# Feed-forward blocks by seven half-size block products, and attention heads with query-major scores and a running-sum instruction, in a two-layer fp32 decoder trunk

## The chip, the cores and the metric

The kernel runs on one core of a Trainium2 chip. The metric is the time of one execution on the device in microseconds (us), the median of several runs. An engine here is one of the core's five: PE is TensorE (matmuls and transposes), DVE is VectorE, ACT is ScalarE, POOL is GpSimd, and SP is SyncE, which issues the loads of weights.

## The reference

Two layers, all in float32, on h of 512 rows and 1024 columns (mem has 256 rows):

```python
for l in range(DEPTH):
    h = h + 0.5 * swiglu_ffn(rms_norm(h, ffn1_norm[l]), ffn1_w_in[l], ffn1_w_out[l])
    h = h + hybrid_mixer(rms_norm(h, mix_norm[l]), w_in[l], conv_w[l], ...)
    h = h + memory_cross_attention(rms_norm(h, xattn_norm[l]), rms_norm(mem, mem_norm[l]), ...)
    h = h + 0.5 * swiglu_ffn(rms_norm(h, ffn2_norm[l]), ffn2_w_in[l], ffn2_w_out[l])
return rms_norm(h, final_norm)

def rms_norm(x, gain, eps=1e-6):
    return x * lax.rsqrt(jnp.mean(x * x, axis=-1, keepdims=True) + eps) * gain
def swiglu_ffn(x, w_in, w_out):            # w_in 1024 x 5632, w_out 2816 x 1024
    gate, up = jnp.split(x @ w_in, 2, axis=-1)
    return (jax.nn.silu(gate) * up) @ w_out
def stick_breaking_attention(q, k, v):     # 8 heads of 64, by blocks of 128 queries
    z = einsum('bhtd,bhsd->bhts', qb, kb) * 64 ** -0.5
    log_beta = log_sigmoid(z)
    log_1m_beta = where(causal, log_beta - z, 0.0)
    between = cumsum(log_1m_beta, axis=3, reverse=True) - log_1m_beta
    a = where(causal, exp(log_beta + between), 0.0)      # then a @ v
```

The mixer projects its input, runs the 8 stick-breaking heads and beside them 4 gated DeltaNet heads of 128 (a causal convolution and silu on q, k, v; l2-normalized q and k; a triangular solve in chunks; a state that goes from chunk to chunk), normalizes each head's output, gates the DeltaNet heads, and projects out.

## The kernel before

Everything lies transposed: columns of h on the partitions, 8 tiles h0 to h7 of 128 x 512. A float32 product is made of three matmuls: each operand is split into a high part (a cast on ScalarE, `split_act`, L164) and a low part (a subtraction on VectorE, `split_low`, L169), and `mm3` multiplies high by high, high by low and low by high. Weights come in units of 128 x 1024 (512 KB): `load` (L171) issues the transfer on SP's queue into one of three raw buffers `wraw`, `unit` (L178) makes the parts `whi` and `wlo` in one of four pairs of buffers, and `take` (L187) hands them to `products` (L199) in the order of a plan, one or more units ahead.

Each layer has four stages: feed-forward, mixer, cross-attention, feed-forward. The order of TensorE's instructions is fixed by the kernel: the stages are written as Python generators, and `weave` (L92) picks among them by a virtual clock. A generator's `yield 3400.0` says that its next part shall not be written before the clock has gone on by so many ns; `yield ("rb",)` waits for a mark; `mm` (L112) moves the clock. The order on the other engines is made by a scheduler, with the DeltaNet thread ahead of others (`urgent`).

*Feed-forward* (`ffn_dense`, L335). The hidden width of 2816 is 22 blocks of 128, in three groups of 8, 8 and 6 (`FGROUPS`). `gate_up` (L340) multiplies a gate unit and an up unit by the 8 tiles of x = h times gain, 512 columns wide. The root 1 / rms of each row is not in x; it is made meanwhile by `rms_rows` (L296) as a tile rb of 128 x 512 (a matmul of ones with the sum of squares, then `newton`, L218, three steps on 512 columns) and applied to the results:

```python
def gated(f, ps):                                            # L350
    nc.vector.tensor_tensor(gt, ps[0], self.rb, op=ALU.mult)     # L352
    nc.scalar.activation(gt, gt, AF.Silu)                        # L353
    nc.vector.tensor_tensor(m, ps[1], gt, op=ALU.mult)           # L355
    self.split_act(hi, m); self.split_low(lo, m, hi)
```

`down` (L367) multiplies a group's m by the 8 units of the output weights, and `add` (L361) scales by rb and adds to h. The next group's first block stands ahead of `down`.

*Mixer* (`mixer`, L912). Four threads share TensorE: the root, the DeltaNet heads one after another (`gdn_head`, L728), the attention heads in pairs (`sb_pair`, L583), and the projections (`mixer_dense`). A DeltaNet head is a chain of short steps on TensorE and VectorE: transposes of k, the root of its length (`rsqrt`, eleven small VectorE steps on 128 x 4), the scaled keys (L771), a triangular solve by levels (1 to 64), then four chunks (L857 on): the product with the state (`rhs`), the product with the solve's result X, its copy `yv` (L870), the new state (L880) and the output. The yields leave room in which the other threads' matmuls stand. An attention head is key-major: scores z lie with keys on the partitions; the sum over later keys is made by TensorE, with a triangle of -1 (`ntri`) and a block of -1 (`nones`, both in tile `cr`) times the split softplus, on top of z in the bank:

```python
t1 = max(z, 0) + Ln(1 + Exp(-|z|)); hi, lo = split(t1)           # scores, L621 to L624
mm(z[...], self.ntri if s2 == s else self.nones, part)           # sums, L630
a = Exp(z); aa = split(a); mm3(av, vpad, aa)                     # weights L642, values
```

*Cross-attention* stands behind the mixer; its memory part is normalized by `mem_norm` (L996) in a thread beside the first feed-forward.

Of the kernel before, what the change touches and what calls it, by code (L numbers as in the profile page):

```python
# [25 lines left out]
P = 128  # L26
# [26 lines left out]
class Trunk:  # L53
# [67 lines left out]
    def setup(self):  # L121
# [23 lines left out]
        self.cr = self.sb([P, 2, P], "cr", F32R)  # L145
        self.cb = self.sb([P, 3, P], "cb", BF16)
        self.ntri, self.nones = (self.cr[:, i, :] for i in range(2))
        self.nsb, self.ngd, self.idb = (self.cb[:, i, :] for i in range(3))
        nc.gpsimd.tensor_copy(self.ntri, stage[:, 0:P])
        nc.gpsimd.tensor_scalar(out=self.nones, in0=self.ones, scalar1=-1.0, scalar2=None, op0=ALU.mult)  # L150
# [36 lines left out]
    def take(self):  # L187

        self.held += 1
        while self.plan and len(self.ahead) < max(1, W_BUFS + 1 - self.held):  # L190
            self.ahead.append(self.unit(self.load(self.plan.pop(0))))
        return self.ahead.pop(0)
# [21 lines left out]
    def rsqrt(self, x, n, tag):  # L214

        return self.newton(x, *(self.sb([P, n], tag + c, bufs=2) for c in "ytm"))

# [92 lines left out]
    G_SLOTS = [f"s{i}" for i in (*range(12, 27), *range(31, 34))]  # L310


    @staticmethod
    def ffn_plan(w_in, w_out):
        r = []
        for i, (f0, f1) in enumerate(FGROUPS):
            if i:
                p0, p1 = FGROUPS[i - 1]
                r += [w_in[f0, 0], w_in[f0, 1]]
                r += [w_out[d][:, p0 * P:p1 * P] for d in range(KD)]  # L320
                f0 += 1
            r += [w_in[f, j] for f in range(f0, f1) for j in range(2)]
        return r + [w_out[d][:, f0 * P - P:f1 * P] for d in range(KD)]
# [3 lines left out]
    def ffn(self, layer, off, *beside, out=None):  # L327
# [5 lines left out]
        self.weave(self.rms_rows(("b6", "b7"), *waits), *beside, self.ffn_dense(x, out is not None))  # L333

    def ffn_dense(self, x, last):  # L335
        nc = self.nc
        banks = [f"b{i}" for i in range(6)]
        g, pend = {}, []

# [10 lines left out]
        def gated(f, ps):  # L350
            gt = self.slot(self.turn("gt", ("s2", "s3")))
            nc.vector.tensor_tensor(gt, ps[0], self.rb, op=ALU.mult)  # L352
            nc.scalar.activation(gt, gt, AF.Silu)  # L353
            m = self.slot(self.turn("m", ("s4", "s5")))
            nc.vector.tensor_tensor(m, ps[1], gt, op=ALU.mult)  # L355
# [4 lines left out]

        def add(d, p, cols=slice(0, S)):  # L361
            h = self.h[d][:, cols]
            t = self.slot(self.turn("up", ("s6", "s7")))[:, cols]
# [3 lines left out]
        def down(f0, f1):  # L367
            d = 0
            xs = [g[f] for f in range(f0, f1)]
            end = f1 == NF  # L370
            while d < KD:
                n = 1 if end and d >= KD - 2 else 2
# [13 lines left out]
                ps = yield from self.products(n, xs, banks)  # L386
# [4 lines left out]
                d += n  # L391

        done = None
        for f0, f1 in FGROUPS:
            yield from gate_up(f0)
            if done:
                yield from down(*done)
            for f in range(f0 + 1, f1):
                yield from gate_up(f)
            done = (f0, f1)  # L400
        yield from down(*done)
# [3 lines left out]
    def final(self, out):  # L405
# [7 lines left out]
        def row(i, r):  # L413
            b = self.bank("rms", banks)
            self.rows(b, r, nt=NT // 2)
            rb = self.slot(("s24", "s25")[i])[:, :S // 2]
# [81 lines left out]
    def gates(self, layer):  # L498
# [36 lines left out]
        yield 12800.0  # L535
# [45 lines left out]
    SBB = (((2, 0, 256),), ((1, 0, 384), (3, 384, 128)), ((0, 0, 512),))  # L581

    def sb_pair(self, layer, pair):  # L583
        nc = self.nc
        mm = self.mm
        t1s = ("s15", "s16", "s17")
        names = [f"s{i}" for i in range(19, 27)]
# [4 lines left out]
        hi, lo = (t.rearrange("p t (j d) -> p t j d", j=3)[:, :, 0:3:2, :] for t in self.vpad)  # L592
        self.split_act(hi, src)
# [674 lines left out]
```

## Time and profile before

| | |
|---|---|
| time, median of 3 runs | 2524.07 us (2523.88 to 2525.02) |
| the profiled execution | 2528.47 us, of which 2526.7 us span |
| mean granted TensorE clock | 0.996 |
| stages on PE, layer 0, from the span's start | 8.4 feed-forward, 373.7 mixer, 736.4 cross-attention, 900.5 feed-forward |
| layer 1 | 1261.5, 1624.0, 1984.9, 2148.6 |

Times in rows are us from the start of the span. "L118" is the matmul in `mm` and "L169" the subtraction in `split_low`, so groups are told apart by tiles: xh, xl are the normalized input's parts, whi and wlo the weights', `b` a PSUM bank (b0 to b5 in feed-forward; in the mixer b6 and b7 are the DeltaNet heads'), `s` a working tile, and f1i, f2o, ... the weights in memory. A busy matmul overlaps the one behind it, so the time that one costs in a run of equal ones is the run's length over their count.

### The profile page before, as it was taken

The numbers are of one execution on the slowest core, as the hardware profiler recorded it, in microseconds if no ns is written. First come the engines' busy times: TensorE is split into PE (matmuls) and PEld (weight loads), VectorE is DVE, ScalarE is ACT, GpSimd is POOL, SyncE is SP. The second block draws the span as 40 slices with busy tenths as digits, with TensorE's granted clock in tenths as the row PEclk, the third lists the DMA queues.
The fourth block names the chain that finished last, engine by engine and source line by source line (L and its number), as shares of the span: only waits on it lengthen the run. The fifth ranks groups of instructions, "written<-read, shape, count | busy, mean of one in ns | idle before, by whom it ended". The sixth has DMA issues, their size and how long they took to land.

```text
span 2526.7 us, 30844 instructions
## 1 busy us (share of the span) xinstructions
PE 2469.2 (98%) x12268; PEld 2070.6 (82%) x12268; DVE 1438.3 (57%) x2585; ACT 970.7 (38%) x1545; POOL 10.5 (0%) x21
## 2 busy tenths in 40 slices
PE   8999999999999999999999999999999999999997
PEld 6888887888889888888888888778888988888886
DVE  6443467788675563444554443687876755544345
ACT  4222236555544432222322222466555444322222
POOL 0000000000000000000000000000000000000000
PEclk9999999999999999999999999999999999999999
DMA  5223232111233123332323222311111432322322
GB/s 192 84 100 100 98 94 67 42 51 36 66 110 125 59 92 100 100 101 88 101 95 98 97 89 94 98 59 42 51 43 51 150 101 67 100 85 99 100 94 65
DMA packets 64672, 220.16 MB, mean 87 GB/s; under 512 B 7312, under 2 KB 9616, under 8 KB 64528
## 3 DMA queue, kind: packets, MB, share of 16 engines
q1 hardware_dynamic: 64096, 217.15, 26.5%
q8 instruction: 96, 1.57, 0.3%
q10 hardware_dynamic: 432, 1.04, 0.1%
q14 instruction: 48, 0.39, 0.0%
HBM read 216.07 MB, written 2.10 MB: 86 GB/s over the span
## 4 chain that ended last, share of the span: by engine, by line
PE 89%; DVE 8%; ACT 1%; issue 1%; DMA 0%; DVEq 0%; SPq 0%; ACTq 0%
PE b L118 88%; DVE wlo L169 2%; PE b L496 1%; DVE s L169 1%; ACT whi L164 1%; DVE qkv L713 1%; DVE s L624 0%; DVE s L810 0%; DVE qk L169 0%; DMA wraw<-f1i 0%; DVE s L822 0%; ACT s L164 0%; DVE s L835 0%; DVE s L836 0%; DVE s L429 0%
## 5 line engine op out<-in xcount | busy, mean ns | idle before, releaser
L118 PE MATMUL b<-xh,whi 128*128 128x512 f32 x2112 | 843.6, 399 | 10.1 <-ACT whi L164 8.4
L118 PE MATMUL b<-xh,wlo 128*128 128x512 f32 x2112 | 826.3, 391 | 0.0
L118 PE MATMUL b<-xl,whi 128*128 128x512 f32 x2112 | 825.7, 391 | 0.2
L164 ACT CAST whi<-wraw 128x1024 fp32r<-128x1024 f32 (+1 forms) x408 | 407.9, 1033 | 1033.5 <-PE b L118 947.6
L118 PE MATMUL b<-s,whi 128*128 128x512 f32 (+1 forms) x2136 | 591.6, 364 | 0.2 <-ACT whi L164 0.2
L169 DVE TENSOR_TENSOR wlo<-wraw,whi 128x1024 fp32r<-128x1024 f32 (+1 forms) x408 | 479.3, 1200 | 72.2 <-ACT whi L164 72.0
L118 PEld LDWEIGHTS b<-xh,whi 128*128 128x128 f32 x2112 | 398.7, 189 | 88.7 <-ACT whi L164 8.4
L118 PEld LDWEIGHTS b<-xh,wlo 128*128 128x128 f32 x2112 | 397.6, 188 | 84.8 <-DVE wlo L169 0.8
L118 PEld LDWEIGHTS b<-xl,whi 128*128 128x128 f32 x2112 | 398.6, 189 | 79.2 <-DVE xl L169 1.5
L118 PEld LDWEIGHTS b<-s,whi 128*128 128x128 f32 x2136 | 382.3, 188 | 64.5 <-issue 0.6
L118 PE MATMUL b<-s,wlo 128*128 128x512 f32 (+1 forms) x1068 | 387.1, 362 | 0.0
L352 DVE TENSOR_TENSOR s<-b,rb 128x512 f32<-128x512 f32 x88 | 60.7, 691 | 450.6 <-PE b L118 450.5
L118 PEld LDWEIGHTS b<-s,wlo 128*128 128x128 f32 x1068 | 201.2, 188 | 32.3
L364 DVE TENSOR_TENSOR s<-b,rb 128x512 f32<-128x512 f32 (+1 forms) x98 | 66.3, 680 | 224.8 <-PE b L118 224.7
L164 ACT CAST s<-s 128x512 fp32r<-128x512 f32 x186 | 107.4, 579 | 158.9 <-DVE s L355 124.6
L169 DVE TENSOR_TENSOR s<-s,s 128x512 fp32r<-128x512 f32 x186 | 118.3, 637 | 65.6 <-ACT s L164 65.2
L118 PEld LDWEIGHTS b<-s,s 128*128 128x128 f32 x656 | 84.6, 191 | 13.1 <-issue 8.1
L118 PE MATMUL b<-s,s 128*128 128x128 f32 (+2 forms) x656 | 86.7, 274 | 3.5 <-DVE rqt L224 1.8
L365 DVE SCALAR_TENSOR_TENSOR h<-s,h 128x512 f32<-128x512 f32 (+1 forms) x98 | 63.0, 673 | 0.0
L353 ACT ACTIVATE s<-s 128x512 f32<-128x512 f32 x88 | 54.9, 625 | 17.6 <-DVE s L352 17.6
L118 PE MATMUL b<-s,cr 128*128 128x128 f32 (+3 forms) x320 | 55.1, 311 | 6.6 <-DVE s L169 6.6
L355 DVE TENSOR_TENSOR s<-b,s 128x512 f32<-128x512 f32 x88 | 60.1, 684 | 1.6 <-ACT s L353 1.4
(240 smaller groups left out, 1820.3 us busy)
## 6 DMA issues: line engine op xcount, KB each, us to landing
wraw<-f1i SPq DMA_DIRECT2D x88, 512.0 KB, 3.7
wraw<-f2i SPq DMA_DIRECT2D x88, 512.0 KB, 3.7
wraw<-wi SPq DMA_DIRECT2D x56, 512.0 KB, 3.5
wraw<-f1o SPq DMA_DIRECT2D x32, 512.0 KB, 3.8
wraw<-xkv SPq DMA_DIRECT2D x32, 512.0 KB, 3.5
wraw<-f2o SPq DMA_DIRECT2D x32, 512.0 KB, 4.2
wraw<-wo SPq DMA_DIRECT2D x16, 512.0 KB, 3.5
wraw<-xq SPq DMA_DIRECT2D x16, 512.0 KB, 3.5
```

What stands on the lines that cost most here:

```text
L118: self.nc.tensor.matmul(out, lhsT, rhs, **kw)
L164: self.nc.scalar.copy(hi, src)
L169: self.nc.vector.tensor_tensor(lo, src, hi.bitcast(F32), op=ALU.subtract)
L352: nc.vector.tensor_tensor(gt, ps[0], self.rb, op=ALU.mult)
L353: nc.scalar.activation(gt, gt, AF.Silu)
L355: nc.vector.tensor_tensor(m, ps[1], gt, op=ALU.mult)
L364: nc.vector.tensor_tensor(t, p, self.rb[:, cols], op=ALU.mult)
L365: nc.vector.scalar_tensor_tensor(out=h, in0=t, scalar=0.5, in1=h, op0=ALU.mult, op1=ALU.add)
L496: self.nc.tensor.transpose(out, src, self.ident[:src.shape[0], :src.shape[0]])
L713: nc.vector.scalar_tensor_tensor(out=y, in0=cv[:, 1 + i:1 + i + S], scalar=w[i], in1=y, op0=ALU.mult, op1=ALU.add)
```

## The change

The feed-forward's input is now also built with the root inside. For blocks 0 to 4 (`WHOLE = 5`) the products are as before, with rb applied to the gate ahead of silu and again behind it. From block 5 on, a block's gate and up (2 x 128 rows of weights), the input's 1024 columns (two halves of 512) and the 512 rows of h (two halves of 256) are taken as a 2 x 2 matrix of blocks each, and the eight block products are made as seven, Strassen's scheme in Winograd's form: p1 = a11 b11, p2 = a12 b21, p5 = s1 t1, p6 = s2 t2, p7 = s3 t3, p3 = s4 b22, p4 = a22 t4. Each is 4 tiles x 3 matmuls of 256 columns. The sums s1 to s4 of weights are made per block on VectorE (`early`: L452 s1, L453 s2, L454 s3, L455 s4) and split; the sums t1 to t4 of the input once per feed-forward (`ffn_parts`). `period` writes product 1 and 2 of block f around products 7, 3 and 4 of block f - 1.

```diff
+    def ffn_parts(self, layer, off):
+        yield ("rb",)
+        for k in range(KD // 2):
+            for j, n in enumerate((n1, n2)):
+                stt(out=n, in0=self.h[k + 4 * j], scalar=self.gain(layer, off, k + 4 * j), in1=self.rb,
+                    op0=ALU.mult, op1=ALU.mult)
+            tt(t3[:, self.HALVES[k % 2]], n2[:, hi], n1[:, hi], op=ALU.subtract)
+            tt(n1[:, hi], n1[:, lo], n1[:, hi], op=ALU.subtract)
+            split(n1, "b11", "t1")
+            split(n2, "b21", "b22")
...
+            yield 3000.0
+        self.mark("parts", 3000.0)
...
+        def early(f):
+            (a11, a12), (a21, a22) = [(r[:, :half], r[:, half:]) for r in raw[f]]
+            hi, lo = self.part(raw[f][0])
...
+            tt(s12[:, :half], a21, a22, op=ALU.add)
+            tt(s12[:, half:], s12[:, :half], a11, op=ALU.add)
+            tt(s3, a11, a21, op=ALU.add)
+            tt(s4, s12[:, half:], a12, op=ALU.add)
+            raw[f] = s12, s3, s4, a22
...
+        def late(f):
+            hi, lo = self.part(raw[f][2], raw[f][3])
...
+        def product(f, left, right, out, start):
+            hi, lo = w[f][left]
+            for k, r in enumerate(self.parts[right]):
+                ks = slice(k * P, (k + 1) * P)
+                self.mm3(out, (hi[:, ks], lo[:, ks]), r, start and k == 0, k == KD // 2 - 1, skip=True)
+                yield 0
...
+        def p3(f):
+            yield from product(f, "s4", "b22", c, False)
+            tt(gt[:, second], c, snap[:, second], op=ALU.add)
+            nc.scalar.activation(gt, gt, AF.Silu)
+        def p4(f):
+            yield from product(f, "a22", "t4", a, False)
+            stt(out=m[:, second], in0=m[:, second], scalar=-1.0, in1=gt[:, second], op0=ALU.mult, op1=ALU.mult)
+            stt(out=m[:, first], in0=a, scalar=-1.0, in1=gt[:, first], op0=ALU.mult, op1=ALU.mult)
+            keep(f, m)
+        def period(f, before, more):
+            yield from p1(f)
+            if before:
+                yield from p7(f - 1)
+            sum3(f)
+            yield from p2(f)
+            if more:
+                early(f + 1)
+            yield from p5(f)
+            yield from p6(f)
+            if more:
+                sums12(f + 1)
+            if before:
+                yield from p3(f - 1)
+                yield from p4(f - 1)
+            late(f)
+            if self.plan and isinstance(self.plan[0], tuple):
+                fetch(f + 2)
         def add(d, p, cols=slice(0, S)):
...
-            nc.vector.tensor_tensor(t, p, self.rb[:, cols], op=ALU.mult)
-            nc.vector.scalar_tensor_tensor(out=h, in0=t, scalar=0.5, in1=h, op0=ALU.mult, op1=ALU.add)
+            stt(out=h, in0=p, scalar=0.5, in1=h, op0=ALU.mult, op1=ALU.add)
```

The root of the rows comes from `rms` instead of `rms_rows`: sums on [128, 4], `newton` there, and four matmuls that spread it to 128 x 512. `down` has product 7 of a group's last block ahead of it and products 3 and 4 behind the first six matmuls of its first unit.

In the mixer the scores are query-major, so that the sum over later keys runs along a row. One VectorE instruction makes it (a scan along reversed columns), a subtraction joins it to z, the weights are transposed on TensorE and split there, and `values` takes two matmuls per tile of keys, with the high and low parts of v side by side, instead of three. `rsqrt_log` takes the place of `rsqrt` in DeltaNet heads (rk, rq, ro) and in the attention heads' norms (sn). Many yields have other numbers.

```diff
+    def rsqrt_log(self, x, n, tag):
+        nc.scalar.activation(y, x, AF.Ln)
+        nc.scalar.activation(y, y, AF.Exp, scale=-0.5)
+        nc.vector.tensor_tensor(t, y, y, op=ALU.mult)
+        nc.vector.scalar_tensor_tensor(out=t, in0=t, scalar=-0.5, in1=x, op0=ALU.mult, op1=ALU.mult)
+        nc.vector.scalar_tensor_tensor(out=y, in0=t, scalar=1.5, in1=y, op0=ALU.add, op1=ALU.mult)
...
+            for t, c, width in bl:
+                back = slice(c + width - 1, c - 1 if c else None, -1)
+                nc.vector.tensor_tensor_scan(out=run[:, back], data0=self.ones[:, 0:1].to_broadcast([P, width]),
+                                             data1=t1[:, back], initial=0.0, op0=ALU.mult, op1=ALU.add)
+            nc.vector.tensor_tensor(t1, z[:, :w], run[:, :w], op=ALU.subtract)
+            nc.scalar.activation(t1, t1, AF.Exp)
...
-                    for part in sp[j, s2]:
-                        mm(z[:, c + (s2 - s) * P:c + width], self.ntri if s2 == s else self.nones, part,
-                           start=False, stop=True, skip_group_check=True)
...
+                    self.transpose(at[i][:, c2:c2 + P], raw[n][:, c + s * P:c + (s + 1) * P])
...
-        rk = self.rsqrt(ss, NT, "rk")
+        rk = self.rsqrt_log(ss, NT, "rk")
...
-            yield 2000.0 if n else 3400.0
+            yield 2200.0 if n else 4200.0
...
-            yield 200.0
+            yield 1000.0
```

VectorE in a feed-forward, before: all that it does for one block (wraw are the loaded weights, b4 and b5 the banks of gate and up, s22 and s23 the parts of m).

```order
L352 TENSOR_TENSOR s3_122_617<-b4_120_566,rb_64_265 128x512
L169 TENSOR_TENSOR wlo_128_629<-wraw_126_626,whi_127_628 128x1024
L169 TENSOR_TENSOR wlo_131_635<-wraw_129_632,whi_130_634 128x1024
L355 TENSOR_TENSOR s5_123_620<-b5_121_567,s3_122_617 128x512
L169 TENSOR_TENSOR s23_125_623<-s5_123_620,s22_124_622 128x512
```

The same engine in one period after (vv holds s1 and s2, vl holds s3, s31 and s32 hold s4; L493 and L508 are additions of two products, L514 and L515 make m):

```order
L165 TENSOR_TENSOR wlo_338_1863<-wraw_328_1811,whi_337_1862 128x1024
L452 TENSOR_TENSOR vv_339_1866<-wraw_329_1813 128x512
L454 TENSOR_TENSOR vl_340_1867<-wraw_328_1811,wraw_329_1813 128x512
L453 TENSOR_TENSOR vv_339_1866<-vv_339_1866,wraw_328_1811 128x512
L493 TENSOR_TENSOR s2_333_1818<-b3_331_1816,s6_332_1817 128x256
L455 TENSOR_TENSOR s31_341_1868<-vv_339_1866,wraw_328_1811 128x512
L508 TENSOR_TENSOR s3_313_1687<-b1_311_1685,s33_312_1686 128x256
L165 TENSOR_TENSOR wlo_343_1901<-vv_339_1866,whi_342_1900 128x1024
L514 SCALAR_TENSOR_TENSOR s5_314_1688<-s5_314_1688,s3_313_1687 128x256
L515 SCALAR_TENSOR_TENSOR s5_314_1688<-b0_310_1684,s3_313_1687 128x256
L165 TENSOR_TENSOR wlo_347_1937<-s32_321_1737,whi_346_1936 128x512
L165 TENSOR_TENSOR wlo_347_1937<-wraw_309_1682,whi_346_1936 128x512
```

Five rows have become fifteen; the low part of one block's a22 (the last row) stands eleven rows behind the sums of the next block. The last two rows' weights wraw_309 are of the block before wraw_328.

TensorE in the fourth DeltaNet head of layer 0, before, from its last level (b7_1070) to the first chunk's product (b6_1075); whi and wlo are units of a projection:

```order
L118 MATMUL b7_1070_5488<-s36_1050_5383,s39_1004_5139 128x128 x4
L118 MATMUL b1_1055_5398<-xh4_456_2576,whi_987_5064 128x512
L118 MATMUL b1_1055_5398<-xl4_457_2577,whi_987_5064 128x512
L118 MATMUL b1_1055_5398<-xh4_456_2576,wlo_988_5065 128x512
L118 MATMUL b1_1055_5398<-xh5_458_2580,whi_987_5064 128x512
L118 MATMUL b1_1055_5398<-xl5_459_2581,whi_987_5064 128x512
L118 MATMUL b1_1055_5398<-xh5_458_2580,wlo_988_5065 128x512
L118 MATMUL b1_1055_5398<-xh6_460_2584,whi_987_5064 128x512
L118 MATMUL b1_1055_5398<-xl6_461_2585,whi_987_5064 128x512
L118 MATMUL b1_1055_5398<-xh6_460_2584,wlo_988_5065 128x512
L118 MATMUL b6_1075_5519<-s32_1000_5120,s36_1050_5383 128x128
```

And after, the same head from its last levels (b7_1200 to b7_1205) through the first chunk (b6_1209 to b7_1214) to the attention head's transposes (L701):

```order
L118 MATMUL b7_1200_6390<-s18_1194_6354,s34_1139_6095 128x128 x4
L118 MATMUL b6_1202_6399<-s39_1145_6116,s36_1193_6353 128x128 x4
L118 MATMUL b7_1203_6405<-s36_1193_6353,s39_1145_6116 128x128 x4
L118 MATMUL b6_1204_6411<-s18_1194_6354,s34_1139_6095 128x128 x4
L118 MATMUL b7_1205_6417<-s36_1193_6353,s39_1145_6116 128x128 x4
L118 MATMUL b6_1209_6432<-s32_1141_6097,s36_1193_6353 128x128
L118 MATMUL b7_1211_6436<-yv_1210_6434,s31_1125_6024 128x128
L118 MATMUL b6_1213_6440<-yv_1210_6434,s35_1140_6096 128x128
L118 MATMUL b7_1214_6443<-st_1212_6438,qkv_976_5341 128x128
L701 MATMUL b2_1216_6447<-cst_13_91,s15_1187_6322 128x128
```

The nine projection matmuls between the last level and the first chunk are gone from there, and the steps of the head stand next to each other.

## Rows read from the trace of the kernel before

**Rows 1.** The page: busy time by engine; share of the chain that ended last.

```profile
PE 2469.2 (98%) x12268; PEld 2070.6 (82%) x12268; DVE 1438.3 (57%) x2585; ACT 970.7 (38%) x1545; POOL 10.5 (0%) x21
...
PE 89%; DVE 8%; ACT 1%; issue 1%; DMA 0%; DVEq 0%; SPq 0%; ACTq 0%
```

**Rows 2.** Windows: us, busy PE, PEld, DVE, ACT, POOL; clock, DMA share, GB/s.

```profile
373.70:736.40 362.70, 345.62 (x1958) 292.06 (x1957) 279.72 (x693) 204.25 (x386) 0.52 (x1) 0.99 0.18 56
900.50:1261.50 361.00, 361.00 (x1587) 297.88 (x1586) 168.27 (x209) 103.82 (x131) 0.00 (x0) 1.00 0.30 96
```

**Rows 3.** The chain in order of time: start, us, what; cross-attention and feed-forward.

```profile
767.07 2.86 PE b L118 x24
...
862.16 751.68 PE b L118 x3301
```

**Rows 4.** Timeline of DVE: start, us, line, operation, tiles, shapes.

```profile
100.69 2.36 DVE L169 TENSOR_TENSOR wlo<-wraw,whi 128x1024 fp32r<-128x1024 f32 x2 [0.21 <-ACT whi L164]
...
422.06 1.22 DVE L169 TENSOR_TENSOR wlo<-wraw,whi 128x1024 fp32r<-128x1024 f32 x1
423.19 0.75 DVE L800 TENSOR_TENSOR s<-b,s 128x256 f32<-128x256 f32 x2
423.86 0.42 DVE L814 TENSOR_TENSOR s<-b,s 128x256 f32<-128x256 f32 x1
...
485.11 0.69 DVE L902 TENSOR_TENSOR s<-s,roy 128x512 f32<-128x512 f32 x1
485.71 0.16 DVE L224 TENSOR_TENSOR rkt<-rky 128x4 f32<-128x4 f32 x1
```

**Rows 5.** Groups by form: busy us, mean ns of one, idle before them.

```profile
L164 ACT CAST whi<-wraw 128x1024 fp32r<-128x1024 f32 x376 | 382.7, 1050 | 953.2 <-PE b L118 872.1 <-issue 76.9 <-DMA wraw<-f1i 2.6
...
L624 DVE SCALAR_TENSOR_TENSOR s<-b,s 128x512 f32<-128x512 f32 x32 | 21.7, 679 | 4.1 <-ACT s L623 4.1
```

**Rows 6.** The page: DMA issues, KB each, median us from issue to landing.

```profile
wraw<-f1i SPq DMA_DIRECT2D x88, 512.0 KB, 3.7
...
wraw<-f2o SPq DMA_DIRECT2D x32, 512.0 KB, 4.2
```

**Rows 7.** Timeline of DVE: first gate after the root in the second-half feed-forward, layer 0.

```profile
919.36 0.69 DVE L352 TENSOR_TENSOR s<-b,rb 128x512 f32<-128x512 f32 x1
```

**Rows 8.** Windows in the first mixer: a wait near 408, one DeltaNet head.

```profile
407.00:411.00 4.00, 2.12 (x12) 1.62 (x11) 2.24 (x7) 3.95 (x4) 0.00 (x0) 0.91 0.30 120
481.00:551.40 70.40, 66.60 (x405) 57.39 (x403) 57.23 (x150) 40.10 (x82) 0.00 (x0) 1.00 0.14 46
```

**Rows 9.** Groups of PE by form, first mixer: the running sums (cr).

```profile
L118 PE MATMUL b<-s,cr 128*128 128x128 f32 x64 | 10.9, 263 | 2.6 <-DVE s L169 2.6
L118 PE MATMUL b<-s,cr 128*128 128x256 f32 x48 | 10.5, 300 | 0.0
L118 PE MATMUL b<-s,cr 128*128 128x384 f32 x32 | 8.9, 362 | 0.0
L118 PE MATMUL b<-s,cr 128*128 128x512 f32 x16 | 6.4, 471 | 0.7 <-DVE s L169 0.7
```

**Rows 10.** Timeline of PE; then the transposes' group by form.

```profile
104.34 0.61 PE L118 MATMUL b<-cst,mny 128*128 128x128 f32 x4
...
766.69 0.38 PE L496 MATMUL b<-cst,s 128*128 128x128 f32 x2
...
L496 PE MATMUL b<-cst,s 128*128 128x128 f32 x192 | 30.1, 274 | 1.1 <-DVE s L989 0.8
```

**Rows 11.** Timeline of DVE: one head's root of the keys.

```profile
483.27 0.17 DVE L220 TENSOR_SCALAR rky<-ss 128x4 int32<-128x4 int32 x1
...
489.13 0.16 DVE L226 SCALAR_TENSOR_TENSOR rky<-rkt,rky 128x4 f32<-128x4 f32 x1
```

**Rows 12.** Timeline of DVE: two steps of a head's chunks.

```profile
541.77 0.35 DVE L880 SCALAR_TENSOR_TENSOR st<-st,eg,b 128x128 f32<-128x128 f32 x1
...
544.92 0.28 DVE L870 COPY yv<-b 128x128 f32<-128x128 f32 x1
```

More of the change, by code (lines that the diff above doesn't have):

```diff
@@ new lines, in p1, with p2 @@
+        def p1(f):
+            a, bc = (self.bank("dense", banks) for _ in range(2))
+            a, b, c = a[:, first], bc[:, first], bc[:, second]
+            snap = self.slot(self.turn("snap", ("s33", "s6")))
+            gt, m = self.slot(self.turn("gt", ("s2", "s3"))), self.slot(self.turn("m", ("s4", "s5")))
+            st[f] = a, b, c, snap, gt, m
+            yield from product(f, "a11", "b11", a, True)
+            nc.scalar.copy(snap[:, first], a)
+        def p2(f):
+            a, b, c, snap, gt, m = st[f]
+            yield from product(f, "a12", "b21", b, True)
@@ new lines, in p5, with p6, p7 @@
+        def p5(f):
+            a, b, c, snap, gt, m = st[f]
+            yield from product(f, "s1", "t1", c, False)
+            nc.scalar.copy(m[:, second], c)
+            tt(gt[:, first], b, snap[:, first], op=ALU.add)
+        def p6(f):
+            a, b, c, snap, gt, m = st[f]
+            yield from product(f, "s2", "t2", a, False)
+            nc.scalar.copy(snap[:, second], a)
+        def p7(f):
+            a, b, c, snap, gt, m = st[f]
+            yield from product(f, "s3", "t3", a, False)
+            tt(m[:, second], a, m[:, second], op=ALU.add)
@@ L391, in down @@
                 d += n
-        done = None
-        for f0, f1 in FGROUPS:
[L395 to L401, printed above, removed]
+                if d == KD - 1 and not end:
+                    self.fill(1)
+                    fetch(left + 1)
+                    early(left + 1)
+        for f in range(self.WHOLE):
+            if f == self.WHOLE - 1:
+                fetch(f + 1)
+            yield from gate_up(f)
+        early(self.WHOLE)
+        sums12(self.WHOLE)
+        fetch(self.WHOLE + 1)
+        yield ("parts",)
+        f = self.WHOLE
+        for f0, f1 in FGROUPS:
+            if f0:
+                sums12(f)
+                fetch(f + 1)
+            end = min(f1, NF - 1)
+            f2 = f
+            while f2 <= end:
+                yield from period(f2, f2 > f, f2 < end)
+                f2 += 1
+            yield from down(f0, f1, end)
+            f = f2
     HALVES = (slice(0, S // 2), slice(S // 2, S))
@@ L645, in values @@
[L645 to L652 removed]
+            self.split_act(hi, at[n][:, :w])
+            self.split_low(lo, at[n][:, :w], hi)
```

289 lines of the change are left out of this document (171 added, 118 removed).

## The prediction

> **What bounds it now.** I read the page's busy times and chain first, then windows of each stage, then single timelines. TensorE works for 98% of the span and the chain of waits lies on it for 89% [rows 1]. Feed-forward stages have no gap at all: 361.00 us busy of 361.00, VectorE 168 us, ScalarE 104 us; a mixer has 345.6 of 362.7 [rows 2]. So a feed-forward stage is worth its matmuls times their spacing, as long as the other engines keep up; a mixer is nearly that, with small waits inside. The spacing is read where long runs of equal matmuls stand in the chain: 3301 of (nearly all) 512 columns in 751.68 us, 0.2277 us each, and 24 of 256 columns in 2.86 us, 0.1192 us each [rows 3]. A 256-column matmul costs 0.52 of a 512-column one, not 0.5. That is the first number which the change depends on.
>
> **The products.** Of the 22 blocks of a feed-forward, 17 change form. Before, a block is 2 x 8 x 3 = 48 matmuls of 512: 48 x 0.2277 = 10.93 us. After, it is 7 x 4 x 3 = 84 of 256: 84 x 0.1192 = 10.01 us. That is 0.92 us a block, and 4 x 17 = 68 blocks: **-62.4 us**. The down products keep their count. [...]
>
> **Does VectorE keep up?** It does the block sums of the weights and more low parts. One period's fifteen instructions (the order's piece shows twelve; the split of m, the add of product 7 and the low part of s3 follow): two of 1024 columns, eight of 512, five of 256. Back to back these take 1.14, 0.60 and 0.33 us from start to start (2.36 less the last one's 1.22; 485.11 to 485.71; 0.75 less 0.42) [rows 4], so 2 x 1.14 + 8 x 0.60 + 5 x 0.33 = 8.73 us of TensorE's 10.01. Laid out with its waits, VectorE stands idle for about 1.2 us per period, at the low part of [a11|a12]: that waits for ScalarE's cast of 1.05 us [rows 5], which may begin when product 2 has freed the weight buffer. The parts are early by some 3 us where TensorE wants them (a11 of the next block lies ready about 6.7 us into the period and is wanted at 10.0). ScalarE has 2 casts of 1024, 4 of 512, a Silu and 3 short copies, under 6 us.
>
> There is a second loop. The up-weights' buffer is held until the low part of a22, and the load into it feeds the next sums (L452) after that. From L452 to the end of a22's low part are 3 x 0.60 + 0.33 + 0.60 + 0.33 + 1.14 + 0.66 + 1.20 + 0.09 = 6.15 us, and a landing takes 3.7 us [rows 6]: 9.9 us against 10.01. Three loops thus stand within 15% of each other; TensorE's is the longest, by little, and the 3 us in hand cover a slightly longer one over runs of 4, 8 and 5 blocks between down products. I take no loss here, and keep the other end for a rival.
>
> **Ends of the feed-forward.** (a) The root for the rows is now made on [128, 4] and spread by four float32 matmul pairs, after four pairs for the sums; a pass costs 0.11 us, (0.61 less 0.27) / 3 [rows 10], so 16 x 0.11 = 1.8 us where the one 512-column pair took about 1.0: +0.8 x 4 = **+3**. (b) The right-hand parts must be built after the root: four rounds, about 4.9 us each on VectorE with their low parts, besides 2.4 us for each whole block's gate. In the built order, 25 to 28 us of VectorE's work stand between the root and the low part of the fifth block's weights. Before, the root was done 18.9 us into the second-half stage (919.36 less 900.5) [rows 2, 7]; after, about 2.5 us earlier, since 512-wide Newton steps go. So 16.5 + 28 = 44.5, wanted at 4 x 10.93 = 43.7. I take 1 to 1.5 us late in each: **+5**. (c) The last block's m is needed six matmuls (1.4 us) after its last product; two short VectorE steps, a cast and a low part are 0.66 + 0.62 + 0.69 + hops, 2.2 us: +0.8 x 4, with small change at the joins **+4**. Feed-forward together: -50.
>
> **The mixers.** Per mixer go the running sums on TensorE, 64, 48, 32 and 16 matmuls of 128, 256, 384 and 512 columns [rows 9]: 64 x 0.11 + 48 x 0.12 + 32 x 0.17 + 16 x 0.23 = 21.9 us, and 8 of each width in the values product, 5.0. 80 transposes come, 0.11 each (0.38 less 0.27) [rows 10]: 8.8. TensorE has **18 us less** to do. But what fills the time between the steps of the DeltaNet heads, one after another, is that same work. Counted in the built order at these spacings, before the first head stand 31.5 us, in the four heads 64.7, 64.0, 64.0, 64.0, and behind them 41.2; in the changed order 26.0, 71.1, 59.5, 64.3, 47.9 and 42.6. A head took 70.4 us with 64.0 of work, so 6.4 of waits [rows 8]. In the fourth head the filling ends early (the order's second piece). From its last levels on, the steps follow each other bare: matmul, 0.8 us to the copied or added result (a copy starts 0.15 us after its matmul ends and takes 0.28, an add 0.35 [rows 12]), three such per chunk, and 1.1 us behind each wide product. That half takes about 23 us; with its filling it took 30. So 16 us of filling taken there give back 7, and the last pair of attention heads, whose transposes, roots and scaling now stand behind the last chunk with nothing beside them, adds about 5.
>
> The roots give something. Before a head's scaled keys (L771) Newton's eleven small steps stand between long ones: from 483.27 to 489.13, 5.9 us, and L771 behind them releases the bank that TensorE waits for [rows 11]. Two ScalarE steps and three on VectorE are 5 instead of 11: I take 2 us a head, -8. With waits as before otherwise: 31.8 + 77.5 + 65.9 + 70.7 + 64.8 + 5 + 43.2 - 8 = 351 against 362.7. I take **-10 a mixer**, both -20.
>
> The scan is in no row. Its ends: 0.60 us for 512 columns, as any two-operand step (the maximum next to it takes 0.679 in all) [rows 4, 5], and 1.14, as a step of twice the columns. As each element needs the one before it, I take the upper end: 8 x (1.14 + 0.87 + 0.33 + 0.60) = 23.5 us a mixer, 10.6 more than at the lower. Beside it go 24 low parts and come 24 subtractions of equal size; the roots take off about as much as the merges add. VectorE's 57.2 of 70.4 us a head [rows 8] rises by some 3. [...]
>
> Sum: -62.4 + 3 + 5 + 4 - 20 = -70. The profiled execution took 2528.5 us (2526.7 of span), 4.4 above the median of 2524.1; 2524 - 70 = **2454 us**.
>
> **Rivals.**
> *The weights' loop binds.* If landings take 4.2 us, as one group does [rows 6], and the steps overlap no more than half (6.6 us), the period is 10.8: 0.8 x 68 less the 3.3 us in hand in each of 12 runs, about +15 to +30. For it: the loops' closeness. Against: loads are spaced, not in pairs. 2465 to 2495.
> *It binds hard, and the kernel is slower.* Place: L452 to a22's low part to the load. The gain of 70 is used up when 68 x e - 40 = 70, e = 1.6, a period of 11.6 us. At full durations (1.22, 0.69, 0.42) the loop is 7.0 us and VectorE's sum 10.06, so it needs landings over 4.6 us in all periods, where most rows say 3.7. 2530 to 2560.
> *The mixers give nothing, or lose.* If VectorE, with the long scans in one queue with the heads' short steps, delays each of these by half a microsecond, some 20 waits a head x 0.5 x 4 heads is 40 us a mixer in which half is hidden: +10 instead of -10. 2475 to 2500. TensorE's clock adds to it: after 2 us of waiting near 408 us its granted clock fell, 0.91 over that stretch [rows 8], and the bare tail waits more.
> [...]
>
> **Chances.** The forecast (2440 to 2470) 0.45; a soft loop 0.18; mixers giving nothing 0.22; faster than 2430 0.07; slower 0.06; within 0.2%, 5 us, which is what a measurement of this kernel can tell from no change, 0.02. From the cases: faster 0.92, same 0.02, slower 0.06. Range 2425 to 2500.
>
> **What would show it.** 256-column matmuls at 0.119 us in the block stretches with TensorE busy over 99%; a period of 10.0 us; VectorE at 85 to 90% there; waits at the fifth block of some us; a fourth head with TensorE idle for over 10 us. Wrong it would be by waits of TensorE for low parts inside the periods, by a load landing late at L452, or by scans ahead of the heads' steps.

## The result and the profile after

The changed kernel takes 2462.33 us (2460.1 to 2464.32, 4 runs) against 2523.98, a ratio of 0.9755 (95% interval 0.9738 to 0.9772). The forecast was 2454, its range 2425 to 2500.

The page of the changed kernel, busy time by engine and the chain's shares, against [rows 1]:

```profile
PE 2394.4 (97%) x14548; PEld 2115.5 (86%) x14548; DVE 1777.2 (72%) x3159; ACT 1182.3 (48%) x2035; POOL 9.1 (0%) x19
...
PE 86%; DVE 11%; ACT 1%; issue 1%; DMA 0%; DVEq 0%; ACTq 0%
```

TensorE has lost 75 us of busy time, VectorE has gained 339, and VectorE's share of the chain went from 8% to 11%. The windows of the changed kernel's stages say where the time came from; columns as in [rows 2].

```profile
8.60:366.90 358.30, 353.86 (x2220) 320.09 (x2221) 261.09 (x428) 169.28 (x266) 3.73 (x6) 1.00 0.33 111
366.90:713.00 346.10, 329.73 (x1845) 273.31 (x1844) 284.60 (x602) 195.31 (x394) 0.00 (x0) 0.99 0.17 58
...
877.20:1228.20 351.00, 348.75 (x2214) 316.84 (x2212) 249.03 (x395) 159.83 (x247) 0.00 (x0) 1.00 0.31 100
1228.20:1579.00 350.80, 348.36 (x2214) 316.78 (x2212) 253.91 (x408) 159.93 (x250) 2.08 (x4) 1.00 0.31 101
1579.00:1927.50 348.50, 332.31 (x1845) 274.84 (x1845) 283.48 (x600) 195.20 (x394) 0.00 (x0) 0.98 0.17 57
...
2091.10:2462.50 371.40, 354.17 (x2265) 323.71 (x2263) 255.27 (x434) 156.40 (x246) 2.82 (x4) 0.97 0.29 93
```

Taken from the stage starts of before, and for the last stage from the spans' ends, the feed-forwards gave 7.0, 10.0, 11.7 and 6.7 us, 35 in all where 50 were forecast. The mixers gave 16.6 and 12.4, 29 where 20 were forecast. Two terms were off by 15 and by 9, in opposite directions; that the sum lies within 9 us of the forecast is in part luck. The cross-attentions are the same within 0.1 us.

A period inside a run of seven-product blocks is read on VectorE's timeline:

```profile
1051.42 1.23 DVE L165 TENSOR_TENSOR wlo<-wraw,whi 128x1024 fp32r<-128x1024 f32 x1 [1.14 <-ACT whi L160]
1052.56 0.68 DVE L452 TENSOR_TENSOR vv<-wraw 128x512 f32<-128x512 f32 x1
...
1058.04 0.69 DVE L165 TENSOR_TENSOR wlo<-wraw,whi 128x512 fp32r<-128x512 f32 x1
...
1061.48 1.22 DVE L165 TENSOR_TENSOR wlo<-wraw,whi 128x1024 fp32r<-128x1024 f32 x1 [1.14 <-ACT whi L160]
1062.62 0.68 DVE L452 TENSOR_TENSOR vv<-wraw 128x512 f32<-128x512 f32 x1
```

From one L452 to the next are 10.06 us: 84 matmuls of 256 columns at 0.1198 each. VectorE's only gap in it is 1.14 us, ahead of the low part that waits for ScalarE's cast. From L452 to the end of a22's low part (1058.04 + 0.69) are 6.17 us. A landing took 3.1 us, by the DMA issues between 1050 and 1075 us:

```profile
wraw<-f2i SPq DMA_DIRECT2D x4, 512.0 KB, 3.1
```

So the loads' loop is 9.3 us long, and TensorE has no gap over three such periods, in which VectorE is busy for 89%:

```profile
1040.00:1070.00 30.00, 30.00 (x253) 30.00 (x252) 26.57 (x46) 18.07 (x30) 0.00 (x0) 1.00 0.29 105
```

At the entry of the blocks TensorE does wait. The chain in order of time in the last feed-forward, at the end of its last whole block and in the first products of the first seven-product block:

```profile
2139.84 9.15 PE b L118 x46
2148.99 0.02 issue
2149.01 0.37 ACT s L483
2149.39 0.54 ACT s L423
...
2149.95 0.69 DVE s L424
...
2151.16 0.69 DVE s L426
2151.85 0.60 DVE vl L454
2152.44 0.60 DVE s L455
...
2153.57 1.23 DVE wlo L165
```

L423 to L426 are the gate of the last whole block (silu, the second factor rb, the product with up); L453 to L455 are the weight sums of the first seven-product block, and the low part at the end is that of s1 and s2. The input's parts are not on this piece of the chain, but they stood ahead of it in VectorE's queue. They begin with L382, which needs the root, here in the second feed-forward (start 877.2) and in the last (start 2091.1):

```profile
896.17 0.75 DVE L382 SCALAR_TENSOR_TENSOR s<-h,gn,rb 128x512 f32<-128x512 f32 x1 [4.88 <-ACT rb L316]
...
2116.47 0.74 DVE L382 SCALAR_TENSOR_TENSOR s<-h,gn,rb 128x512 f32<-128x512 f32 x1
```

That is 19.0 and 25.4 us after the stage's start. From just before it VectorE works without a gap until the low part is done:

```profile
2114.20:2155.00 40.80, 36.88 (x177) 30.83 (x176) 40.77 (x69) 22.35 (x34) 0.00 (x0) 0.98 0.17 58
```

Windows around the entries, of the first, second and last feed-forward:

```profile
45.00:90.00 45.00, 41.31 (x237) 35.91 (x236) 41.28 (x80) 21.65 (x36) 0.00 (x0) 0.96 0.17 59
925.00:945.00 20.00, 18.56 (x116) 16.52 (x115) 18.39 (x28) 9.77 (x16) 0.00 (x0) 1.00 0.28 95
...
2150.00:2160.00 10.00, 6.08 (x30) 5.67 (x29) 9.26 (x14) 3.47 (x6) 0.00 (x0) 0.68 0.16 52
```

TensorE stands still for 3.7, 1.4 and 3.9 us there, and the granted clock of these stretches is 0.96 and 0.68 in the first and the last. Part of each ran at a granted clock of 0.50 (61.5 to 64.0 us and 2155.3 to 2160.1), with 512-column matmuls 0.427 us apart in the first, where they stood 0.227 apart ahead of the waits, and 256-column ones 0.213 apart in the last, against 0.1198. In the third feed-forward no such wait is listed.

In the mixer, windows from each DeltaNet head's first transposes to the next one's, and the stretch behind the fourth:

```profile
401.40:468.70 67.30, 65.81 (x385) 54.96 (x385) 60.39 (x121) 42.09 (x82) 0.00 (x0) 1.00 0.16 56
468.70:533.90 65.20, 62.57 (x377) 52.63 (x377) 59.71 (x129) 38.94 (x84) 0.00 (x0) 1.00 0.17 57
533.90:603.00 69.10, 68.01 (x410) 57.73 (x410) 59.44 (x130) 40.26 (x88) 0.00 (x0) 1.00 0.14 47
603.00:662.60 59.60, 52.37 (x314) 43.89 (x315) 48.07 (x111) 35.71 (x81) 0.00 (x0) 0.97 0.16 54
662.60:713.00 50.40, 46.47 (x205) 37.29 (x204) 31.02 (x55) 19.56 (x33) 0.00 (x0) 0.93 0.20 63
```

The first three heads take 65 to 69 us where one took 70.4 [rows 8]. The fourth is shorter, but TensorE stands for 7.2 us in it and 3.9 behind it, at a falling clock. The scan, by form on VectorE:

```profile
L828 DVE TENSOR_TENSOR_SCAN s<-cst,s 128x512 f32<-128x512 f32 x16 | 19.5, 1220 | 0.2
...
L828 DVE TENSOR_TENSOR_SCAN s<-cst,s 128x128 f32<-128x128 f32 x16 | 6.5, 406 | 0.0
```

1220 ns for 512 columns is what a subtraction of 1024 takes (1221 ns, L165), the upper end that the prediction took.

### The profile page after: what moved, and what is told of

It reads as the page before. It is cut to its first block, busy times and chain, and to the rows that moved or that the text cites. A ratio compares the mean times of both kernels' runs of the same rounds, so it can differ in the third digit from the quotient of the medians.

```text
span 2462.5 us, 36398 instructions
## 1 busy us (share of the span) xinstructions
PE 2394.4 (97%) x14548; PEld 2115.5 (86%) x14548; DVE 1777.2 (72%) x3159; ACT 1182.3 (48%) x2035; POOL 9.1 (0%) x19
## 4 chain that ended last, share of the span: by engine, by line
PE 86%; DVE 11%; ACT 1%; issue 1%; DMA 0%; DVEq 0%; ACTq 0%
PE b L118 84%; PE b L701 1%; DVE wlo L165 1%; DVE qkv L914 1%; DVE s L828 1%; DVE s L823 1%; ACT whi L160 1%; DVE s L165 1%; DVE s L830 0%; DVE s L1042 0%; DVE s L382 0%; DMA wraw<-f1i 0%; DVE s L1011 0%; DVE s L1051 0%; DVE s L424 0%
## 5 line engine op out<-in xcount | busy, mean ns | idle before, releaser
L118 PE MATMUL b<-s,whi 128*128 128x256 f32 (+1 forms) x3064 | 658.2, 306 | 3.6 <-ACT whi L160 2.2
L160 ACT CAST whi<-wraw 128x1024 fp32r<-128x1024 f32 (+2 forms) x408 | 387.2, 959 | 505.4 <-PE b L118 449.3
L118 PE MATMUL b<-xh,whi 128*128 128x512 f32 (+1 forms) x1552 | 583.5, 401 | 14.7 <-ACT whi L160 8.6
L165 DVE TENSOR_TENSOR wlo<-wraw,whi 128x1024 fp32r<-128x1024 f32 (+2 forms) x408 | 450.6, 1110 | 142.4 <-ACT whi L160 140.8
L118 PE MATMUL b<-xl,whi 128*128 128x512 f32 x1472 | 548.2, 393 | 2.6 <-DVE xl L165 1.7
L118 PE MATMUL b<-xh,wlo 128*128 128x512 f32 (+1 forms) x1288 | 505.0, 392 | 2.4 <-DVE wlo L165 2.3
L118 PE MATMUL b<-s,wlo 128*128 128x256 f32 (+1 forms) x1532 | 467.3, 305 | 3.5 <-DVE wlo L165 3.5
L118 PE MATMUL b<-qk,whi 128*128 128x256 f32 (+1 forms) x1152 | 234.1, 290 | 0.0
L118 PEld LDWEIGHTS b<-qk,whi 128*128 128x128 f32 x1152 | 182.1, 192 | 2.4
L118 PE MATMUL b<-qk,wlo 128*128 128x256 f32 (+1 forms) x576 | 166.8, 290 | 0.0
L160 ACT CAST whi<-vv 128x1024 fp32r<-128x1024 f32 x68 | 71.4, 1050 | 130.0 <-issue 71.4
L118 PEld LDWEIGHTS b<-s,s 128*128 128x128 f32 x656 | 84.5, 194 | 25.4 <-DVE s L1042 10.4
```

The costliest lines, as they stand in the source:

```text
L118: self.nc.tensor.matmul(out, lhsT, rhs, **kw)
L160: self.nc.scalar.copy(hi, src)
L165: self.nc.vector.tensor_tensor(lo, src, hi.bitcast(F32), op=ALU.subtract)
```

## The experiments

**The feed-forwards alone** (2488.23 us, 2486.59 to 2489.47; ratio to before 0.9856, 0.9841 to 0.987). The kernel before with the feed-forward of after:

```diff
-        self.weave(self.rms_rows(("b6", "b7"), *waits), *beside, self.ffn_dense(x, out is not None))
+        self.weave(self.rms(("b6", "b7"), *waits), *beside, self.ffn_parts(layer, off),
+                   self.ffn_dense(x, out is not None))
...
-        self.vpad = [self.sb([P, NT, 192], n, F32R) for n in ("vph", "vpl")]
+        big, small = self.sb([P, 1024], "vph", F32R), self.sb([P, 576], "vpl", F32R)
```

> The feed-forwards of after, the mixers and cross-attention of before (the padded values tile is cut in two pieces to make room for the weight sums). By the stages of the two traces the feed-forwards got 35 us shorter by themselves: about 2489 us, the mixers 362 us each as before. If the prediction's sum were right and the profiled run of after only had bad luck, -50: 2474. If the two halves of the change help or hurt each other over VectorE or the loads, the number lies outside 2485 to 2493.

**The mixers alone** (2497.82 us, 2496.68 to 2502.21; 0.9897, 0.9883 to 0.9912). The kernel after with the feed-forward of before:

```diff
-        self.weave(self.rms(("b6", "b7"), *waits), *beside, self.ffn_parts(layer, off),
-                   self.ffn_dense(x, out is not None))
+        self.weave(self.rms_rows(("b6", "b7"), *waits), *beside, self.ffn_dense(x, out is not None))
```

> The mixers of after, the feed-forwards of before. By the stages of the traces the mixers give 16.5 and 12.4, 29 us: about 2495 us. By the prediction's term, -20: 2504. If the shorter mixers come from the feed-forward ahead of them (what it leaves loaded or queued), less than 20: above 2504.

The medians are 36.7 and 27.1 below their before (2524.94), 63.8 together, and both changes in one kernel gave 61.7: the halves are independent to within some 2 us, and the two mis-sized terms can be looked at one by one.

**The root of the last feed-forward sooner** (2455.63 us, 2454.16 to 2457.18; 0.9727, 0.9711 to 0.9744).

```diff
-        waits = (13000.0, 6000.0) if beside else (8000.0, 6000.0)
+        waits = (13000.0, 6000.0) if beside and out is None else (8000.0, 6000.0)
```

> After, with one number changed: in the last feed-forward the root's thread waits 8 us at its start, as in the two inner ones, not 13. Theory: the waits of 6.9 us at its fifth block (and the clock that falls there) come from input parts that are built too late since the root is late by 5 us: they shrink to 0 to 3 us, the whole by 4 to 6 us, to about 2457. Rival: VectorE has too much to do in the whole blocks in any case, and the parts come when it is through: within 1 us of after.

6.7 us below after, and no run of either overlaps the other. The last stage alone is 6.8 us shorter, 364.6 where it was 371.4:

```profile
2088.90:2453.50 364.60, 351.22 (x2265) 321.14 (x2263) 255.24 (x434) 156.59 (x246) 2.81 (x4) 0.98 0.30 94
```

The written wait had put the first step of the root later there, by 5 us as written. Timelines of VectorE in after, the second feed-forward (start 877.2) and the last (2091.1):

```profile
887.21 0.17 DVE L243 TENSOR_SCALAR rny<-ms 128x4 int32<-128x4 int32 x1
...
2107.24 0.17 DVE L243 TENSOR_SCALAR rny<-ms 128x4 int32<-128x4 int32 x1
```

That is 10.0 us after the stage's start in the one, 16.1 in the other. In the run with 8 us TensorE has no gap at the place of the waits; windows of that kernel:

```profile
2133.00:2143.00 10.00, 10.00 (x46) 8.29 (x45) 10.00 (x17) 4.93 (x7) 0.00 (x0) 1.00 0.32 105
2143.00:2153.00 10.00, 10.00 (x77) 9.61 (x76) 9.98 (x16) 5.61 (x10) 0.00 (x0) 1.00 0.17 54
```

Its first feed-forward is that of after, and it has the same 3.7 us of waits between 45 and 90 us, but there the clock stayed at 1.00, not 0.96:

```profile
45.00:90.00 45.00, 41.31 (x249) 36.32 (x248) 42.93 (x84) 21.91 (x37) 0.00 (x0) 1.00 0.17 59
```

**The rows' spreading sooner everywhere** (2457.53 us, 2457.46 to 2460.08; 0.9737, 0.9722 to 0.9751).

```diff
-        waits = (13000.0, 6000.0) if beside else (8000.0, 6000.0)
+        waits = (13000.0, 2500.0) if beside and out is None else (8000.0, 2500.0)
```

> As the run before, and the second wait of the root's thread, between the sums and the spreading to the rows, is 2.5 us instead of 6 in all four feed-forwards, so that the parts can begin 3.5 us sooner. Theory: the waits at the fifth block (5.5, 3.0, 0.3 and 6.9 us in after) are gone or under 2 us in all: 8 to 13 us below after, about 2452. Rival: VectorE's amount of work decides: as the run before, or TensorE waits for the root's Newton steps at the spreading instead, and gives some us back there.

Here the theory failed: the time is 4.8 us below after, and no better than with the last root alone. (The waits that it names, 5.5, 3.0 and 6.9 us, are larger than the 3.7, 1.4 and 3.9 of the windows above.) The first feed-forward became 360.8 us instead of 358.3, and the second won under 1 us. What TensorE waits for between 45 and 90 us, in after and in this run:

```profile
PE b L118 <- DVE wlo L165: 3.7, 3, 1.5
```

```profile
PE b L118 <- DVE wlo L165: 4.3, 3, 2.1
```

These are low parts of weights. The input's parts began 3.7 us sooner (32.5 us against 36.2), and in this kernel's timeline they and three steps of the gate fill VectorE from 48.6 us to 59.3, ahead of the low part that TensorE waits for. So an earlier spreading does not help the first feed-forward. That the place of the parts in VectorE's queue is the reason is read from the timeline; no run changes it alone. The first wait of 13 us was left as it is in the first feed-forward in every run.

**More work for VectorE where it stands idle** (2463.72 us, 2462.51 to 2466.01; 0.9759, 0.9745 to 0.9774).

```diff
         def sum3(f):
             w[f]["s3"] = self.part(raw[f][1])
+            for _ in range(2):
+                self.split_low(w[f]["s3"][1], raw[f][1], w[f]["s3"][0])
```

> After, and VectorE writes the low part of s3 three times instead of once: 1.2 us more work per period (68 of them), beside the loads' loop. Theory: VectorE has 8.73 of 10.06 us and stands idle for 1.14 in one piece ahead of the next low part; 9.93 still fits, periods stay at 10.06 us and the time within 3 us of after (2462). Rival: where VectorE's idle time stands matters, its short steps come late for the products, and each period pays some of the 1.2: 10 to 60 us more.

**More work between the sums and the load** (2562.5 us, 2559.63 to 2566.09; 1.015, 1.0135 to 1.0165).

```diff
+            tt(s3, a11, a21, op=ALU.add)
+            tt(s3, a11, a21, op=ALU.add)
+            tt(s3, a11, a21, op=ALU.add)
+            tt(s3, a11, a21, op=ALU.add)
             tt(s3, a11, a21, op=ALU.add)
```

> After, and the sum s3 is computed five times instead of once: 2.4 us more of VectorE's time per period, all of it between the first sum and the low part of a22, after which the next load starts. VectorE's work is then 11.13 us and the loads' loop 7.9 + 3.1 = 11.0. Theory: the period is 11.1 to 11.2 us, 1.1 x 68 = 73 us less what the parts' lead of 3 us covers in each of 12 runs of blocks: about 2500 us, and up to 2535 without the lead. Rival: the scheduler's order lets TensorE go on (weights are two blocks ahead) and the time moves by under 10 us.

The first is free, as forecast: the window from 1040 to 1070 us of that kernel shows VectorE busy for all but 0.2 us and TensorE without a gap.

```profile
1040.00:1070.00 30.00, 30.00 (x253) 30.00 (x253) 29.83 (x51) 17.71 (x31) 0.00 (x0) 1.00 0.29 101
```

The second costs 100 us, more than both answers. VectorE's timeline in that kernel (L459 and L454 to L458 are its sums, columns as above):

```profile
1119.83 0.69 DVE L454 TENSOR_TENSOR vl<-wraw,wraw 128x512 f32<-128x512 f32 x1
...
1130.24 1.23 DVE L165 TENSOR_TENSOR wlo<-wraw,whi 128x1024 fp32r<-128x1024 f32 x1 [0.91 <-ACT whi L160]
...
1131.98 0.69 DVE L454 TENSOR_TENSOR vl<-wraw,wraw 128x512 f32<-128x512 f32 x1
```

The period is 12.15 us, not 11.1: VectorE's 11.13 of work and a wait for the cast, still 0.91, make 12.04. (68 periods longer by 2.09, less 3 us of lead in each of 12 runs of blocks, would be 106 us.) Even here VectorE stands idle for 0.91, so the room in a period of 10.06 is not 10.06 less 8.73; work at another place than the gap has, by this estimate, only 10.06 - 8.73 - 0.9, some 0.4 us. The gain of 62 us turned into a loss of 38, which is the outcome of the rival "it binds hard", but not its place: between 1100 and 1160 us L452 waited for a landing once, for 1.3 us.

**Long roots again** (2494.52 us, 2492.56 to 2497.54; 0.9878, 0.9861 to 0.9894).

```diff
-        rk = self.rsqrt_log(ss, NT, "rk")
+        rk = self.rsqrt(ss, NT, "rk")
```

and the same for rq, ro and sn.

> After, with Newton's eleven steps again in place of the logarithm, the exponential and three steps, at all four places in the mixers. The prediction's term: 2 us a head, 8 a mixer: about 2478 us. Rival: the root is hidden behind other work, or the two ScalarE steps wait as long as the Newton steps did: within 4 us of 2462.

32 us, twice the forecast. In the first head TensorE waits 2.4 us for the scaled keys (L972 in this kernel), as it waited for them in before and not in after:

```profile
PE b L118 <- DVE s L972: 2.4, 1, 2.4
```

A part of the loss there is the clock, at 0.91 over that head:

```profile
399.90:477.20 77.30, 71.88 (x385) 60.19 (x385) 62.36 (x137) 41.51 (x78) 0.00 (x0) 0.91 0.15 48
```

It takes 77.3 us instead of 67.3; the other heads of that mixer and the stretch behind them lose 1.4 to 3.5 each.

**The short root alone, in the kernel before** (2515.07 us, 2513.93 to 2516.14; 0.9957, 0.9942 to 0.9972).

```diff
-        rk = self.rsqrt(ss, NT, "rk")
+        rk = self.rsqrt_log(ss, NT, "rk")
```

and the same for rq, ro and sn.

> Before, with the short root (logarithm, exponential, three steps) in the mixers as its only change; all waits written between the steps as before. Theory: each head's scaled keys come 2 us sooner, and the waits of 6.4 us a head fall by up to 2: 4 to 8 us a mixer, 2508 to 2516 us. Rival: the written waits are cut to the long root, so that the order on TensorE leaves no room to use it: within 4 us of before (2525).

11.2 us below its before (2526.24), 5.6 a mixer. What TensorE waited for over the first four heads of before and of this kernel, the longest of each:

```profile
PE b L118 <- DVE s L771: 4.9, 3, 1.7
PE b L118 <- DVE s L169: 4.4, 9, 0.8
```

```profile
PE b L118 <- DVE s L169: 3.5, 9, 0.7
PE b L507 <- ACT qkv L726: 1.9, 1, 1.9
```

The waits for the scaled keys (L771, L782 in this kernel) are gone, by the mechanism that the prediction named.

**The old waits between the heads' steps** (2519.96 us, 2516.05 to 2522.84; 0.9981, 0.9972 to 0.999).

```diff
-        yield 2600.0
+        yield 3400.0
...
-            yield 2200.0 if n else 4200.0
+            yield 2000.0 if n else 3400.0
...
-            yield 500.0 if n > len(small) else 3300.0
+            yield 900.0 if n > len(small) else 2200.0
...
-            yield 1000.0
+            yield 200.0
```

and five more such numbers in the gates and heads.

> After, with the waits that the DeltaNet heads and their gates write between their steps set back to the numbers of before: other work is put between the steps at other places, nothing else. Theory: the heads' waits fell from 6.4 to 3.2 to 5.7 us since the shorter roots and these numbers fit each other, so that the old numbers give some of that back: 4 to 15 us more than after. Rival: the waits are set by VectorE's queue, not by where filling stands: within 3 us.

58 us, far over the theory and its rival, from numbers that only say where work of other threads is written between the steps. The longest wait of TensorE between 470 and 622 us there:

```profile
PE b L701 <- DVE s L898: 10.0, 2, 5.0
```

TensorE comes twice to a group of transposes (L701) 5 us before VectorE has scaled an attention pair's output by its root (L898); that step stands in VectorE's queue behind steps of a DeltaNet head and of the projections. It shows a mismatch of order and steps, not what the new numbers would be worth by themselves.

**The scores alone** (2546.05 us, 2543.65 to 2548.68; 1.0076, 1.0059 to 1.0093): the last kernel and the long roots together.

```diff
-        rk = self.rsqrt_log(ss, NT, "rk")
+        rk = self.rsqrt(ss, NT, "rk")
...
-            yield 2200.0 if n else 4200.0
+            yield 2000.0 if n else 3400.0
```

> After, with both the long roots and the old waits between the steps of the DeltaNet heads: of the change in the mixers the query-major scores are left alone. Theory: what went from TensorE was filling between the steps of the heads, and without shorter steps the 18 us less of work a mixer give nothing: mixers of 358 to 366 us, 2487 to 2502 us. Rival: the two losses of the single runs (32 and 58 us) add up, since each moves a step of the chain: about 2550.

The rival was right and the theory wrong: the losses add up (84 of 90 us). Its first mixer in one window:

```profile
365.10:755.70 390.60, 352.16 (x1846) 289.26 (x1845) 298.61 (x730) 192.93 (x363) 0.00 (x0) 0.92 0.16 51
```

390.6 us against 362.7 in before [rows 2], with fewer matmuls and a clock of 0.92.

**Every running sum twice** (2507.35 us, 2505.96 to 2508.49; 0.9926, 0.9911 to 0.9941).

```diff
+                nc.vector.tensor_tensor_scan(out=run[:, back], data0=self.ones[:, 0:1].to_broadcast([P, width]),
+                                             data1=t1[:, back], initial=0.0, op0=ALU.mult, op1=ALU.add)
                 nc.vector.tensor_tensor_scan(out=run[:, back], data0=self.ones[:, 0:1].to_broadcast([P, width]),
                                              data1=t1[:, back], initial=0.0, op0=ALU.mult, op1=ALU.add)
```

> After, and every running sum is computed twice (the same values to the same place): 23.5 us more of VectorE's time a mixer, in one queue with the short steps of the DeltaNet heads. Theory: VectorE is busy for 285 of 346 us there and the scans delay some of the heads' steps: 5 to 15 us more a mixer, 2472 to 2492 us. Rival: the heads' steps go first and the second scans are hidden: within 4 us of after (2462).

45 us for 47 us of added VectorE work: nearly none of it is hidden, and the time lies above both answers. A part is again the clock, 0.90 in the fourth head. Windows of its second and fourth head:

```profile
471.60:542.80 71.20, 64.47 (x377) 53.10 (x377) 65.54 (x137) 38.29 (x84) 0.00 (x0) 0.99 0.16 52
...
618.20:685.50 67.30, 56.55 (x314) 46.71 (x315) 53.73 (x119) 35.67 (x81) 0.00 (x0) 0.90 0.15 47
```

**Root and memory** (2454.82 us, 2453.96 to 2455.18; 0.9718, 0.9703 to 0.9732), the fastest.

```diff
-        waits = (13000.0, 6000.0) if beside else (8000.0, 6000.0)
+        waits = (13000.0, 6000.0) if beside and out is None else (8000.0, 6000.0)
...
     def mem_norm(self):
-        yield 16000.0
+        yield 100000.0
```

> The last feed-forward's root at 8 us as in the run with 2455.6 us, and the squares of the memory's normalization beside the first feed-forward start at 100 us instead of 16, behind its entry. Theory: the waits of 4.2 us at the fourth and fifth block of the first feed-forward come from VectorE's amount of work there (spreading the root sooner only moved them), so 3 us less work takes 2 to 4 of them: about 2453 us. Rival: they come from the late root alone: no change, 2455 to 2457.

It stands within the interval of the run with the root alone (0.9711 to 0.9744), and between 45 and 90 us TensorE still waits 3.2 us for low parts of weights. Moving that work away gave at most a microsecond, so it is hardly what TensorE waits for in that entry; what would take those waits away stays open.

## Why the prediction was right

**The products.** Forecast -62.4. A block took 10.06 us instead of 10.01, since the 256-column matmuls stand 0.1198 us apart and not 0.1192: 68 x (10.93 - 10.06) is -59.

**VectorE and the loads.** Forecast 8.73 us of work, 1.2 of idling and a loop of 9.9 us, all inside 10.01. Measured: 8.9 of work (10.06 less the gap), 1.14 of idling and 9.3 for the loop, since a landing took 3.1 and not 3.7. No loss was right. The added sums showed how narrow the room beside it is, narrower than VectorE's busy share says.

**The ends of the feed-forward.** This step was mis-sized: "I take 1 to 1.5 us late in each", +5 in all. The working took the root at 16.5 us after the start for all four. The input's parts, which need it, began at 19.0 in the second and at 25.4 in the last. The first and the last have a thread beside them, so the root's thread waits 13 us there instead of 8, which stands in the code; setting the last to 8 gave back 6.7 us. In place of the 5 us stand 9 us of waits (3.7, 1.4, none, 3.9) and some 4 us of low clock (an estimate from the spacing at either level, 1.7 in the first and 2.6 in the last). With -59 for the products that leaves some 11 us, against 7 forecast for the root's matmuls and the joins, which were not measured by themselves. Why the first feed-forward waits stays open: spreading the root sooner and moving the memory's work away both left its waits.

**The mixers.** Forecast -20, measured -29. The first took 346.1 us against 351. By stretches, the start and the first head took 101.8 us where 107.3 were forecast (31.8 + 77.5 less 2 for the root), the second and third head 134.3 for 132.6, the fourth and what is behind it 110.0 for 111.0. So the tail was right: the fourth head lost its filling, and TensorE stands in it and behind it for 11 us. The gain beyond the forecast lies ahead of the second head, where TensorE stands for only 1.5 us. What failed is the phrase "with waits as before otherwise". (The 6.4 us a head that it carries on are time less counted work; in [rows 8] TensorE is without a matmul for 3.8.) The new numbers between the steps got no term, and with the old ones this kernel loses 58 us; which of the nine numbers does it was not tried.

The roots were right in kind: the waits for the scaled keys went, and 5.6 us a mixer came of it in the old kernel (forecast 8), 16 in the new one. With long roots and the new numbers the kernel takes 2494.5 us, no less than the 2488.2 of the feed-forwards alone; with long roots and the old numbers, a mixer with 18 us less work for TensorE is 28 us slower. "TensorE has 18 us less to do" thus describes the change in work, and is not by itself the cause of the gain: the 29 us came of the scores, the short roots and the numbers together.

The scan's time was right: the trace has 1220 ns for 512 columns, and 682 for the maximum beside it. The reason given for the upper end, that each element needs the one before it, is the author's; no run shows why the scan takes longer. A second one costs nearly all of its time (45 of 47 us); the one scan lies on the chain with 1.0% of the span, some 25 of its 52 us.

**The rivals.** The soft loop and the hard loop did not come, nor did a time below 2430: the fastest execution of the changed kernel took 2460.1 us. "The mixers give nothing" did not come either, but its mechanism, scans in one queue with short steps, costs 22 us a mixer at twice the scans.

## What to carry to other kernels

When a saving lies on an engine that is 98% busy, what decides is whether a second engine can carry the work moved to it: lay out one period of that engine with its waits, since an idle piece that waits for another engine's cast is room only at its own place (here 0.91 us stayed idle even in periods of 12.15). Where a program fixes one engine's order by hand, what a shorter step is worth depends on how the work between the steps is laid out (here 5.6 us a mixer in one layout, 16 in another); forecast these numbers as a term of their own. When a term is worked out in one copy of a stage, read the arguments of the other copies.

## What the runs showed of the hardware

A short wait of TensorE cost more than its length in one place. In the last feed-forward, over the 10 us that hold 3.9 us of waits, the granted clock was 0.68, and the run without these waits was 6.7 us faster. It was not so each time: with the same 3.7 us of waits in the first feed-forward the clock was 0.96 in the trace of after and 1.00 in that of the run with the last root sooner. In the mixer of the scores alone the clock was 0.92 over all 390.6 us, in the first mixer of after 0.99.

A scan of 128 x 512 took 1220 ns on VectorE, where a maximum of the same size took 682.
